# The low parts of the weights in three tiles that begin 128, 256 and 384 bytes past a multiple of 512

## The chip, the cores and the metric

The kernel runs on one NeuronCore of a Trainium2 chip. What counts is the device time of one execution, in microseconds (us). Engines are named as the profile names them: PE is the matrix engine (its matmuls; PEld are its weight loads), DVE the vector engine, ACT the scalar engine, POOL the GpSimd engine, SP the engine that here only issues DMAs. SBUF is the on-chip memory of 128 partitions from which all engines read. Addresses below are bytes within a partition.

## The reference

A decoder trunk of two layers on 256 tokens of width 2048, all in float32:

```
for i in range(2):
    hn = rmsnorm(h, norm_mix[i])
    mix = pool_mixer(hn) if i == 0 else diff_attention(hn)      # layer 0: trailing means and 4 products of 512x512
    h = h + mix                                                 # layer 1: w_qkv [2048, 6144], 8 heads, w_o [2048, 2048]
    hn = rmsnorm(h, norm_ffn[i])
    h = h + (silu(hn @ w_gate[i]) * (hn @ w_up[i])) @ w_down[i] # 2048 -> 5632 -> 2048
return rmsnorm(h, final_norm)
```

Nearly all the work is in the matrix products, and their weights are read once from memory.

## The kernel before

A product in float32 is made of products in a faster, shorter format, `float32r`. A weight block of 128 x 2048 numbers (`raw`, 1 MB, one DMA on SP's queue) is split in `halves` (lines 105 to 110): ACT copies it, rounded, to the high part `whi` (line 108), and DVE subtracts that from `raw` and writes the low part `wlo` (line 109). Activations are split in the same way when they are made, and stay in SBUF as `xp`, `h` or `oT`. A product is then three matmuls: activation high with weight high, activation high with weight low, activation low with weight high. In `group` (line 162), the activations, 128 columns, are the loaded, stationary operand, and 512 columns of `whi` or `wlo` are streamed past it, the moving operand. In `product` (lines 419 and 421, for the queries and keys) it is the other way round: 128 columns of `whi` or `wlo` are loaded and 512 or 256 columns of an activation stream. Each matmul has a weight load of its own.

There are 331 weight blocks: 3 for the pooling mixer, 176 for `w_gu` (the gate and up products), 88 for `w_down`, 32 for `w_qk`, 16 each for `w_v` and `w_o`. Three buffers each of `raw`, `whi` and `wlo` let the DMA, the split and the matmuls of successive blocks run side by side. In three of the eight pairs of row tiles (`SEVEN`), a gate and up product takes seven block products in place of eight; it needs sums of the weight blocks, made on DVE as `tsum` (lines 114 to 117) and split to `thi` and `tlo` (lines 120 and 121), which have one buffer each.

The order of the instructions on each engine is set by the scheduler of the framework in which the kernel is written, which also hands out a pool's buffers in the order in which it thinks they come free. So `whi` and `wlo` of one block always got buffers of the same place in their pools, and the places mostly went round in threes; once in each feed-forward layer, at its sixth block, the block took again the place of the block just before it.

Every large tile of the program as built begins at a multiple of 512 bytes: `raw` at 65024, 73216 and 81408, `whi` at 89600, 97792 and 105984, `wlo` at 114176, 122368 and 130560, and so do `xp`, `h`, `oT`, `tsum`, `thi`, `tlo` and the blocks of 2048 bytes in them that a matmul streams. Some small tiles of the attention do not: `q_c`, `k_s`, `s_sb` and `bias` begin 224 bytes past a multiple of 512, `o_n` 288 past, `a_sb` 32 past.

Of the kernel before, what the change touches and what calls it, by code (L numbers as in the profile page):

```python
# [9 lines left out]
F32 = mybir.dt.float32  # L10
F32R = mybir.dt.float32r
# [5 lines left out]
P = 128  # L17
# [27 lines left out]
def trunk_kernel(ctx, tc, x_t, x_n, gains, scale_in, final_in, subln, lam_in, band, dist,  # L45
# [15 lines left out]
    whl = ctx.enter_context(tc.tile_pool(name="whl", bufs=3))  # L61
# [3 lines left out]
    turn = {"acc": 0, "aux": 0}  # L65
# [8 lines left out]
    def aux(shape=(P, 512)):  # L74
        turn["aux"] += 1
        return bank(5 + turn["aux"] % 3, shape)
# [19 lines left out]
    def f32(ap):  # L96
        return ap.bitcast(F32)


    def load(src):  # L100
        raw = wraw.tile([P, 4, 512], F32, name="raw")
        nc.sync.dma_start(out=raw, in_=src)
        return raw

    def halves(raw, lo_block=0):
        hi = whl.tile([P, 4, 512], F32R, name="whi")
        lo = whl.tile([P, 4, 512], F32R, name="wlo")
        nc.scalar.copy(hi[:, lo_block:], raw[:, lo_block:])  # L108
        nc.vector.tensor_tensor(lo[:, lo_block:], raw[:, lo_block:], f32(hi[:, lo_block:]), ALU.subtract)  # L109
        return hi, lo  # L110
# [17 lines left out]
    def group(steps, seven_pool=None):  # L128
# [15 lines left out]
        for (a, seven, src), step in zip(steps, plan):  # L144
            raw = load(src)
            w = [halves(raw, B11 if seven else 0)]
            if seven:
                w.append(sums(seven_pool, raw))
            for b, parts in step:
                first = b not in ps  # L150
                if first:
                    ps[b] = bank(b)
                for at, which, block in parts:
                    hi, lo = w[which]
                    if seven:
                        ah, al = a[:, 0, at], a[:, 1, at]
                    else:
                        k, t = at
                        ah, al = (a[:, k, i, t * P:(t + 1) * P] for i in range(2))
                    for x, y in ((ah, hi), (ah, lo), (al, hi)):  # L160
                        left[b] -= 1
                        nc.tensor.matmul(ps[b], x, y[:, block], start=first, stop=(left[b] == 0))  # L162
                        first = False
# [235 lines left out]
    with tc.tile_pool(name="attn", bufs=1, reuse_waits="tile") as ap_, ExitStack() as heads:  # L399
        at = heads.enter_context(tc.tile_pool(name="attn_tmp", bufs=2, reuse_waits="tile"))  # L400
# [13 lines left out]
        def product(src, acts):  # L414

            ps = acc((P, 2, S))
            hi, lo = (x.rearrange("p b (u n) -> p (b u) n", n=P) for x in halves(load(src)))
            for k, a in enumerate(acts):
                big = lambda: nc.tensor.matmul(ps.rearrange("p a s -> p (a s)"), hi[:, k], a.rearrange("p a s -> p (a s)"),  # L419
                                               start=(k == 0), stop=(k == NK - 1))  # L420
                small = lambda: nc.tensor.matmul(ps[:, 0, :], lo[:, k], a[:, 0, :], start=False, stop=False)  # L421
                if k < NK - 1:
                    big()
                    small()
                else:
                    small()
                    big()
            return ps

        def transpose_probs(h, probs):  # L430

            a_t = ap_.tile([P, 2, S], F32, name=f"aT{h}")
            tr_ps = aux()
            for qb in range(2):
                for kb in range(qb + 1):
                    o0 = kb * S + qb * P
                    nc.tensor.transpose(tr_ps[:, o0:o0 + P], probs[qb][:, kb * P:(kb + 1) * P], ident)
            nc.scalar.copy(a_t[:, 0, :], tr_ps[:, 0:S])
            nc.scalar.copy(a_t[:, 1, P:], tr_ps[:, S + P:])
            aT.append(a_t)  # L440
# [3 lines left out]
        for h in range(H):  # L444

            if h:
                qk = ap_.tile([P, 4, S], F32, name=f"qk{h}", tag="qk", bufs=8)
            for i in range(4):
                ps = product(w_qk[h * 4 + i], acts)
                if i == 1 and probs is not None:  # L450
                    transpose_probs(h - 1, probs)
                if r is None:
                    bc = aux()
                    for t in range(2):
                        nc.tensor.matmul(bc[:, t * P:(t + 1) * P], r_col[:, t:t + 1].broadcast_to([P, P]), ident,
                                         start=True, stop=True)
                    r = ap_.tile([P, S], F32, name="r_row")
                    nc.scalar.copy(r, bc[:, :S])

                    lp = ap_.tile([P, 2], F32, name="lp")  # L460
                    nc.vector.tensor_tensor(lp, lam_sb[:, 0:2], lam_sb[:, 2:4], ALU.mult)
                    l_ps = aux()
                    nc.tensor.matmul(l_ps[:, 0:2], ones, lp, start=True, stop=True)
                    le = ap_.tile([P, 2], F32, name="le")
                    nc.scalar.activation(le, l_ps[:, 0:2], AF.Exp)
                    neg_lam = ap_.tile([P, 1], F32, name="neg_lam")
                    nc.vector.scalar_tensor_tensor(neg_lam, le[:, 1:2], -LAMBDA_INIT, le[:, 0:1], ALU.add, ALU.subtract)
                    gs = ap_.tile([P, 2], F32, name="gs")
                    nc.vector.tensor_scalar(gs, subln_sb, 1.0 - LAMBDA_INIT, None, ALU.mult)
                c = at.tile([P, S], F32, name="q_c")  # L470
                nc.scalar.copy(c, ps[:, 1, :])
                if i < 2:
                    nc.vector.tensor_tensor(qk[:, i, :], ps[:, 0, :], c, ALU.add)
                else:
                    s = at.tile([P, S], F32, name="k_s", bufs=1)
                    nc.vector.tensor_tensor(s, ps[:, 0, :], c, ALU.add)
                    nc.vector.tensor_tensor(qk[:, i, :], s, r, ALU.mult)
            bias = at.tile([P, 2 * P], F32, name="bias")
            nc.vector.tensor_scalar(bias, dist_sb, -(2.0 ** (-8.0 * (h + 1) / H)), None, ALU.mult)
            probs = []  # L480
            for qb in range(2):
                nk = (qb + 1) * P
                b_ap = bias[:, P:] if qb == 0 else bias
                ps_t, inv = [], []
                for c in range(2):
                    sc = aux()
                    nc.tensor.matmul(sc[:, :nk], qk[:, c, qb * P:(qb + 1) * P], qk[:, 2 + c, :nk], start=True, stop=True)  # L487
                    s = at.tile([P, S], F32, name="s_sb", bufs=3)
                    nc.vector.scalar_tensor_tensor(s[:, :nk], sc[:, :nk], qs_col[:, qb:qb + 1], b_ap, ALU.mult, ALU.add)
                    m = at.tile([P, 1], F32, name="m_neg", bufs=3)  # L490
                    nc.vector.tensor_reduce(m, s[:, :nk], AX.X, ALU.max, negate=True)
                    p = at.tile([P, S], F32, name="p_sb", bufs=4)
                    l = at.tile([P, 1], F32, name="l_sum", bufs=3)
                    nc.scalar.activation(p[:, :nk], s[:, :nk], AF.Exp, bias=m, accum_out=l)
                    iv = at.tile([P, 1], F32, name="l_inv", bufs=4)
                    nc.vector.reciprocal(iv, l)
                    ps_t.append(p)
                    inv.append(iv)
                nc.vector.tensor_tensor(inv[1], inv[1], neg_lam, ALU.mult)
                p1 = at.tile([P, S], F32, name="p1_sb")  # L500
                nc.vector.tensor_scalar(p1[:, :nk], ps_t[1][:, :nk], inv[1], None, ALU.mult)
                a = at.tile([P, S], F32, name="a_sb")
                nc.vector.scalar_tensor_tensor(a[:, :nk], ps_t[0][:, :nk], inv[0], p1[:, :nk], ALU.mult, ALU.add)
                probs.append(a)
        transpose_probs(H - 1, probs)
        heads.close()
        at = heads.enter_context(tc.tile_pool(name="out_tmp", bufs=2, reuse_waits="tile"))
# [132 lines left out]
```

## Time and profile before

| | before |
|---|---|
| median of 3 runs | 1916.08 us (1915.61 to 1916.73) |
| the profiled execution, its own time | 1915.97 us |
| its span, first to last instruction | 1914.2 us |
| PE busy | 1871.7 us, 98% |
| DVE busy | 1344.9 us, 70% |
| ACT busy | 921.3 us, 48% |
| DMA | 358.83 MB, 187 GB/s over the span |

Matmuls overlap in the profile: one of 512 columns is shown some 390 ns long, while the next begins some 227 ns after it. How fast PE works is read from the starts of its matmuls, in the timeline, not from the mean length of one.

### The profile page before, as it was taken

How to read it: one execution, taken by the hardware profiler on the slowest of the kernel's cores; microseconds unless marked ns; L12 is line 12 of the kernel's file. 1: busy time of each engine (PE TensorE's matmuls, PEld its weight loads, DVE VectorE, ACT ScalarE, POOL GpSimd, SP SyncE). 2: the span in 40 equal slices, each digit the busy share in tenths (PEclk: the TensorE clock that was granted, in tenths of full speed). 3: DMA queues.
4: the chain of work that ended last, by engine and by line, in shares of the span. 5: the costliest groups of instructions: out<-in, count | busy, mean ns of one | idle time of the engine just before them, and what ended most of it. 6: DMA issues, size and time to landing. Idle time of an engine off the chain costs nothing.

```text
span 1914.2 us, 20836 instructions
## 1 busy us (share of the span) xinstructions
PE 1871.7 (98%) x8508; PEld 1526.5 (80%) x8508; DVE 1344.9 (70%) x1311; ACT 921.3 (48%) x892; POOL 0.7 (0%) x6
## 2 busy tenths in 40 slices
PE   8899999999999999999999999999999999999997
PEld 5678888888888888888887787788888888888886
DVE  5898756888558975666654356898558897468854
ACT  5555534455434545544445545555434554345543
POOL 0000000000000000000000000000000000000000
PEclk9999999999999999999999999999999999999999
DMA  7455555555556564555553454555555556565552
GB/s 284 154 198 198 197 180 198 195 198 198 195 188 211 176 207 169 177 174 177 174 186 137 139 176 157 189 203 199 198 195 201 198 176 211 185 219 198 198 194 92
DMA packets 51151, 358.83 MB, mean 187 GB/s; under 512 B 6000, under 2 KB 6256, under 8 KB 8432
## 3 DMA queue, kind: packets, MB, share of 16 engines
q1 hardware_dynamic: 50080, 355.36, 53.3%
q10 hardware_dynamic: 976, 2.15, 0.3%
q8 instruction: 66, 1.08, 0.2%
q14 instruction: 29, 0.24, 0.0%
HBM read 355.39 MB, written 2.10 MB: 187 GB/s over the span
## 4 chain that ended last, share of the span: by engine, by line
PE 93%; DVE 3%; ACT 2%; DMA 1%; issue 1%; SPq 0%; DVEq 0%; ACTq 0%
PE b L162 80%; PE b L419 6%; PE b L421 3%; PE b L357 1%; DVE wlo L109 1%; ACT whi L108 1%; DMA x_tok<-x_n 1%; PE b L297 1%; PE b L487 1%; ACT sq L212 0%; PE b L533 0%; PE b L307 0%; DVE xp L224 0%; DMA raw<-w_gu 0%; ACT o_sq L525 0%
## 5 line engine op out<-in xcount | busy, mean ns | idle before, releaser
L109 DVE TENSOR_TENSOR wlo<-raw,whi 128x2048 fp32r<-128x2048 f32 (+1 forms) x331 | 721.3, 2182 | 354.8 <-ACT whi L108 354.0
L108 ACT CAST whi<-raw 128x2048 fp32r<-128x2048 f32 (+1 forms) x331 | 603.1, 1825 | 607.6 <-PE b L162 511.1
L162 PE MATMUL b<-whi,xp 128*128 128x512 f32 x2412 | 768.4, 392 | 6.5 <-DVE xp L224 3.9
L162 PEld LDWEIGHTS b<-whi,xp 128*128 128x128 f32 x2412 | 453.2, 188 | 104.4 <-issue 5.1
L162 PE MATMUL b<-wlo,xp 128*128 128x512 f32 x1206 | 470.7, 390 | 1.8 <-DVE wlo L109 1.8
L162 PE MATMUL b<-whi,h 128*128 128x512 f32 x1408 | 438.3, 391 | 0.0
L162 PEld LDWEIGHTS b<-whi,h 128*128 128x128 f32 x1408 | 263.7, 188 | 56.8 <-DVE h L360 2.1
L162 PE MATMUL b<-wlo,h 128*128 128x512 f32 x704 | 274.2, 390 | 0.1
L162 PEld LDWEIGHTS b<-wlo,xp 128*128 128x128 f32 x1206 | 226.9, 188 | 50.0 <-DVE wlo L109 3.0
L121 DVE TENSOR_TENSOR tlo<-tsum,thi 128x2048 fp32r<-128x2048 f32 x66 | 151.1, 2290 | 52.6 <-ACT thi L120 51.7
L162 PE MATMUL b<-thi,xp 128*128 128x512 f32 x528 | 185.1, 397 | 2.4 <-ACT thi L120 2.3
L419 PE MATMUL b<-xp,whi 128*128 128x512 f32 x512 | 183.1, 402 | 0.0
L120 ACT CAST thi<-tsum 128x2048 fp32r<-128x2048 f32 x66 | 126.1, 1910 | 99.5 <-DVE tsum L117 77.0
L162 PEld LDWEIGHTS b<-wlo,h 128*128 128x128 f32 x704 | 132.2, 188 | 27.3 <-DVE wlo L109 0.5
L421 PE MATMUL b<-xp,wlo 128*128 128x256 f32 x512 | 138.0, 280 | 0.0
L162 PEld LDWEIGHTS b<-thi,xp 128*128 128x128 f32 x528 | 97.2, 189 | 28.7 <-ACT thi L120 10.9
L419 PEld LDWEIGHTS b<-xp,whi 128*128 128x128 f32 x512 | 95.0, 188 | 19.8
L162 PE MATMUL b<-tlo,xp 128*128 128x512 f32 x264 | 105.4, 399 | 0.0
L421 PEld LDWEIGHTS b<-xp,wlo 128*128 128x128 f32 x512 | 96.6, 189 | 2.6
L162 PE MATMUL b<-whi,oT 128*128 128x512 f32 x256 | 81.5, 397 | 0.5 <-DVE xp L224 0.5
L114 DVE TENSOR_TENSOR tsum<-raw 128x1024 f32<-128x1024 f32 x66 | 80.5, 1220 | 0.6
L162 PEld LDWEIGHTS b<-tlo,xp 128*128 128x128 f32 x264 | 50.0, 189 | 13.7 <-DVE tlo L121 3.2
(122 smaller groups left out, 1016.7 us busy)
## 6 DMA issues: line engine op xcount, KB each, us to landing
raw<-w_gu SPq DMA_DIRECT2D x176, 1024.0 KB, 4.8
raw<-w_down SPq DMA_DIRECT2D x88, 1024.0 KB, 4.8
raw<-w_qk SPq DMA_DIRECT2D x32, 1024.0 KB, 4.8
raw<-w_v SPq DMA_DIRECT2D x16, 1024.0 KB, 4.8
raw<-w_o SPq DMA_DIRECT2D x16, 1024.0 KB, 4.8
raw<-pool_w SPq DMA_DIRECT2D x3, 1024.0 KB, 16.9
x_tok<-x_n SPq DMA_DIRECT2D x1, 2048.0 KB, 14.2
xf<-x_t SPq DMA_DIRECT2D x3, 512.0 KB, 10.8
```

What stands on the lines that cost most here:

```text
L108: nc.scalar.copy(hi[:, lo_block:], raw[:, lo_block:])
L109: nc.vector.tensor_tensor(lo[:, lo_block:], raw[:, lo_block:], f32(hi[:, lo_block:]), ALU.subtract)
L114: nc.vector.tensor_tensor(t[:, T1:T3 + 1], raw[:, B11:B22 + 1], raw[:, B12:B12 + 1].broadcast_to([P, 2, 512]), ALU.add)
L120: nc.scalar.copy(hi, t)
L121: nc.vector.tensor_tensor(lo, t, f32(hi), ALU.subtract)
L162: nc.tensor.matmul(ps[b], x, y[:, block], start=first, stop=(left[b] == 0))
L297: nc.tensor.matmul(zp[g][t], u, w[:, k % 4], start=(k % 4 == 0 and i == 0), stop=(k % 4 == 3 and i == 2))
L357: nc.tensor.transpose(tp[:, k, t * P:(t + 1) * P], h[:, t, (2 * i + k) * P:(2 * i + k + 1) * P], ident)
L419: big = lambda: nc.tensor.matmul(ps.rearrange("p a s -> p (a s)"), hi[:, k], a.rearrange("p a s -> p (a s)"), start=(k == 0), stop=(k == N ...
L421: small = lambda: nc.tensor.matmul(ps[:, 0, :], lo[:, k], a[:, 0, :], start=False, stop=False)
L487: nc.tensor.matmul(sc[:, :nk], qk[:, c, qb * P:(qb + 1) * P], qk[:, 2 + c, :nk], start=True, stop=True)
```

## The change

The three buffers of `wlo` become three tiles with a tag of their own, used in turn, and gaps of 128 bytes stand before each of them and behind the last. As built, `wlo_a`, `wlo_b` and `wlo_c` begin at 114304, 122624 and 130944, which is 128, 256 and 384 bytes past a multiple of 512. `raw` and `whi` stay where they were. What lies behind (from `ss` on) moves up by 512 bytes, so that it keeps its place within 512. To make room, the attention's `bias` has one buffer in place of two.

```
+    turn["lo"] = 0
+
     def halves(raw, lo_block=0):
         hi = whl.tile([P, 4, 512], F32R, name="whi")
-        lo = whl.tile([P, 4, 512], F32R, name="wlo")
+        i = turn["lo"] % 3
+        turn["lo"] += 1
+        if turn["lo"] <= 3:
+            whl.tile([P, 32], F32, name=f"gap{i}", tag=f"gap{i}", bufs=1)
+        lo = whl.tile([P, 4, 512], F32R, name="wlo_" + "abc"[i], tag=f"wlo{i}", bufs=1)
+        if turn["lo"] == 3:
+            whl.tile([P, 32], F32, name="gap3", tag="gap3", bufs=1)
         nc.scalar.copy(hi[:, lo_block:], raw[:, lo_block:])
         nc.vector.tensor_tensor(lo[:, lo_block:], raw[:, lo_block:], f32(hi[:, lo_block:]), ALU.subtract)
         return hi, lo
...
-            bias = at.tile([P, 2 * P], F32, name="bias")
+            bias = at.tile([P, 2 * P], F32, name="bias", bufs=1)
```

No instruction is added or removed. The order on the engines is the same but for three places: DVE's `bias` instructions, one a head, come one head later but for the first (still ahead of their readers), and at the start of each feed-forward layer the sixth block's low part, which now goes strictly in turn, gets the buffer of the third block before it instead of the one just freed. There the scheduler puts the low part behind the sums. In the first feed-forward layer DVE's rows were these before (the number at the end of a name is a buffer's; `wlo_644` is the sixth block's, `tsum_612`, `thi_616` and `tlo_617` are the sums of the fifth):

```order
L109 TENSOR_TENSOR wlo_644<-raw_641,whi_643 128x2048 [waits DMAHW4_49,Activation_49]
L114 TENSOR_TENSOR tsum_612<-raw_606 128x1024 [waits DVE_49]
L116 TENSOR_TENSOR tsum_612<-tsum_612,raw_606 128x512 [waits DVE_49]
L117 TENSOR_TENSOR tsum_612<-tsum_612,raw_606 128x512 [waits DVE_49]
L109 TENSOR_TENSOR wlo_674<-raw_671,whi_673 128x2048 [waits DMAHW5_49,Activation_49]
L121 TENSOR_TENSOR tlo_617<-tsum_612,thi_616 128x2048 [waits Activation_49]
L109 TENSOR_TENSOR wlo_704<-raw_701,whi_703 128x2048 [waits DMAHW6_49,Activation_49]
```

And they are these now (numbers of buffers are higher by 4, of lines by 9):

```order
L123 TENSOR_TENSOR tsum_616<-raw_610 128x1024 [waits DVE_49]
L125 TENSOR_TENSOR tsum_616<-tsum_616,raw_610 128x512 [waits DVE_49]
L126 TENSOR_TENSOR tsum_616<-tsum_616,raw_610 128x512 [waits DVE_49]
L118 TENSOR_TENSOR wlo_c_648<-raw_645,whi_647 128x2048 [waits DMAHW4_49,PE_49,Activation_49]
L130 TENSOR_TENSOR tlo_621<-tsum_616,thi_620 128x2048 [waits Activation_49]
L118 TENSOR_TENSOR wlo_a_678<-raw_675,whi_677 128x2048 [waits DMAHW5_49,PE_49,Activation_49]
L118 TENSOR_TENSOR wlo_b_708<-raw_705,whi_707 128x2048 [waits DMAHW6_49,Activation_49]
```

The low part stands three rows later, behind the sums, and it and the next one now wait for PE too, for the matmuls that read their buffers last. PE's rows at the same place before:

```order
L162 MATMUL b5_506<-whi_578,xp_94 128x512
L162 MATMUL b6_486<-wlo_644,xp_96 128x512 [waits DVE_49]
L162 MATMUL b6_486<-whi_643,xp_96 128x512 x2
L162 MATMUL b6_486<-wlo_644,xp_96 128x512
L162 MATMUL b6_486<-whi_643,xp_96 128x512
L162 MATMUL b4_502<-wlo_644,xp_96 128x512
L162 MATMUL b4_502<-whi_643,xp_96 128x512 x2
L162 MATMUL b4_502<-wlo_644,xp_96 128x512
L162 MATMUL b4_502<-whi_643,xp_96 128x512
L162 MATMUL b7_569<-wlo_644,xp_96 128x512
L162 MATMUL b1_490<-thi_616,xp_95 128x512 [waits Activation_49]
```

And now:

```order
L171 MATMUL b5_510<-whi_582,xp_94 128x512
L171 MATMUL b1_494<-thi_620,xp_95 128x512 [waits Activation_49]
L171 MATMUL b2_498<-thi_620,xp_95 128x512
L171 MATMUL b3_502<-thi_620,xp_95 128x512
L171 MATMUL b5_510<-thi_620,xp_95 128x512
L171 MATMUL b6_490<-wlo_c_648,xp_96 128x512 [waits DVE_49]
L171 MATMUL b6_490<-whi_647,xp_96 128x512 x2
L171 MATMUL b6_490<-wlo_c_648,xp_96 128x512
L171 MATMUL b6_490<-whi_647,xp_96 128x512
L171 MATMUL b4_506<-wlo_c_648,xp_96 128x512
L171 MATMUL b4_506<-whi_647,xp_96 128x512 x2
```

The four matmuls on `thi` have moved ahead of those on the low part. The second feed-forward layer has the same exchange at the same place.

## The prediction

> **What bounds the kernel now.** I read the page's head first, then its chain of waits, then the groups.
>
> ```profile
> PE 1871.7 (98%) x8508; PEld 1526.5 (80%) x8508; DVE 1344.9 (70%) x1311; ACT 921.3 (48%) x892; POOL 0.7 (0%) x6
> PE 93%; DVE 3%; ACT 2%; DMA 1%; issue 1%; SPq 0%; DVEq 0%; ACTq 0%
> L109 DVE TENSOR_TENSOR wlo<-raw,whi 128x2048 fp32r<-128x2048 f32 (+1 forms) x331 | 721.3, 2182 | 354.8 <-ACT whi L108 354.0
> L108 ACT CAST whi<-raw 128x2048 fp32r<-128x2048 f32 (+1 forms) x331 | 603.1, 1825 | 607.6 <-PE b L162 511.1
> L162 PE MATMUL b<-wlo,xp 128*128 128x512 f32 x1206 | 470.7, 390 | 1.8 <-DVE wlo L109 1.8
> L162 PE MATMUL b<-wlo,h 128*128 128x512 f32 x704 | 274.2, 390 | 0.1
> L421 PE MATMUL b<-xp,wlo 128*128 128x256 f32 x512 | 138.0, 280 | 0.0
> ```
>
> PE is the bound: 98% busy, 93% of the chain. ACT waits 511.1 us for PE to free `whi`, so the split runs ahead of PE and is paced by it. PE's matmuls on `wlo` waited 1.8 us in all for DVE. A faster or slower line 109 would therefore be hidden; only two things can move the end: the pace of a matmul itself, and the few places where PE waits.
>
> The pace is read from the starts in the timeline of PE's rows. In the steady stretch from 270 to 290 us the groups and the first and last low matmul are:
>
> ```profile
> L162 PE MATMUL b<-whi,h 128*128 128x512 f32 x60 | 18.6, 389 | 0.0
> L162 PE MATMUL b<-wlo,h 128*128 128x512 f32 x30 | 11.7, 389 | 0.0
> 269.86 0.39 PE L162 MATMUL b<-wlo,h 128*128 128x512 f32 x1
> ...
> 289.58 0.39 PE L162 MATMUL b<-wlo,h 128*128 128x512 f32 x1
> ```
>
> There are 30 low matmuls, every third one, so 29 x 3 = 87 matmuls lie between the two starts: 19.72 us / 87 = 226.7 ns. What would the 512 columns alone take? Just after PE's longest wait the granted clock is 0.50 (column after POOL's), and the starts in that stretch give the pace at half clock:
>
> ```profile
> 66.00:68.50 2.50, 2.50 (x7) 1.92 (x7) 1.74 (x7) 1.41 (x2) 0.00 (x0) 0.50 0.26 39
> 66.10 0.63 PE L162 MATMUL b<-wlo,xp 128*128 128x512 f32 x1
> 67.38 0.63 PE L162 MATMUL b<-wlo,xp 128*128 128x512 f32 x1
> 68.66 0.49 PE L162 MATMUL b<-wlo,xp 128*128 128x512 f32 x1
> ```
>
> Six matmuls in 2.56 us, 427 ns each, so 213 ns at full clock. The steady pace is 13.3 ns above that. The excess looks as if it belongs to the weight load, not to the columns: in the queries and keys, where 512 and 256 columns alternate, nine pairs go by in 3.12 us:
>
> ```profile
> 866.67 0.28 PE L421 MATMUL b<-xp,wlo 128*128 128x256 f32 x1
> ...
> 869.79 0.28 PE L421 MATMUL b<-xp,wlo 128*128 128x256 f32 x1
> ```
>
> That is 346.7 ns a pair; 768 columns at 213/512 ns are 320, and 26.7 ns are left for two matmuls, again 13.3 each. And the next weight load runs while the columns stream: at 280.06 us the low matmul and a weight load start together.
>
> ```profile
> 280.06 0.39 PE L162 MATMUL b<-wlo,h 128*128 128x512 f32 x1
> 280.06 0.41 PEld L162 LDWEIGHTS b<-whi,h 128*128 128x128 f32 x2
> ```
>
> So some 13.3 ns of each such matmul are lost to something that the half clock leaves room for. Whether that depends on where in 512 bytes the two reads begin is the whole question, because before, both always begin at 0.
>
> **The change part by part.** *PE reading `wlo` at 128, 256, 384.* In the trace of before no matmul streams a tile that is off a multiple of 512, so this has no row of its own. Low bound: the excess goes away wherever one of the two reads is of `wlo`. These are the 1206 and 704 above, 128 more and 24 of the mixer:
>
> ```profile
> L162 PE MATMUL b<-wlo,oT 128*128 128x512 f32 x128 | 50.4, 394 | 0.0
> L297 PE MATMUL b<-wlo,xp 128*128 128x512 f32 x24 | 10.3, 430 | 1.6 <-DVE wlo L109 1.6
> ```
>
> together 2062 that stream it, and 512 that load it: 2574 x 13.3 ns = 34 us less. High bound: a second excess of the same size, 34 us more; I know no steady row with a larger one. I take 0, for three rows that stand nearest. First, loads of a stationary operand off 512 are in the trace: the transposes of `a_sb` (32 past) have the length of those of `h` (0 past).
>
> ```profile
> L357 PE MATMUL b<-ident,h 128*128 128x128 f32 x176 | 28.6, 278 | 0.1
> L437 PE MATMUL b<-ident,a_sb 128*128 128x128 f32 x24 | 4.1, 272 | 0.0
> ```
>
> They are plain float32, at less than one column a cycle, so they leave the room that the half clock leaves; they weigh little. Second, other engines read and write at 224 and 288 past at the speed of aligned work of the same size: 420 against 420 ns on DVE (line 476 against 245), 474 against 475 on ACT (line 529 against 223).
>
> ```profile
> L476 DVE TENSOR_TENSOR k_s<-b,q_c 128x256 f32<-128x256 f32 x16 | 6.7, 420 | 14.5 <-ACT q_c L471 14.5
> L245 DVE TENSOR_TENSOR e<-e 128x256 f32<-128x256 f32 x6 | 2.5, 420 | 2.3 <-ACT e L243 2.3
> L529 ACT ACTIVATE o_n<-b,rs_r 128x256 f32<-128x256 f32 x16 | 6.5, 474 | 1.5 <-DVE rs_r L206 1.5
> L223 ACT ACTIVATE oT<-b,gs 128x256 fp32r<-128x256 f32 x16 | 7.4, 475 | 3.8 <-PE b L533 2.3 <-DVE oT L224 1.5
> ```
>
> Third, if the engines met in banks of the SBUF that the address selects, PE's pace would move with what DVE and ACT do. In two stretches of 10 us, with DVE busy 9.71 and 4.59, PE starts the same number of matmuls:
>
> ```profile
> 610.00:620.00 10.00, 10.00 (x46) 8.29 (x45) 9.71 (x8) 3.73 (x4) 0.00 (x0) 1.00 0.67 225
> 1040.00:1050.00 10.00, 10.00 (x46) 8.27 (x45) 4.59 (x2) 4.60 (x3) 0.00 (x0) 1.00 0.31 105
> ```
>
> The loss is thus PE's own, between its two reads, and most simply a shared way in, whatever the address.
>
> The Trainium skill goes further ("TensorE: Matmul & The Clock Gate", Part 2, step 1): it gives PE two independent SBUF read ports, and says that the next load takes no read bandwidth from the running matmul. By it the sum for this part is 0 and no address can matter. The trace agrees that the load runs beside the matmul, but not that it is free at full clock: 226.7 against 213 ns.
>
> *DVE writing `wlo`.* By the same DVE rows, nothing per instruction; and what it might cost is covered by the slack before line 108. Should that cover go, each 1% of 721.3 us is 7 us of DVE time, still under 98% of PE.
>
> *The order at the start of each feed-forward layer.* The sixth block's low part must now wait until PE has read the third block's low part for the last time. Before, in the first of the two layers:
>
> ```profile
> 82.33 2.29 DVE L109 TENSOR_TENSOR wlo<-raw,whi 128x2048 fp32r<-128x2048 f32 x1
> 85.88 0.39 PE L162 MATMUL b<-wlo,xp 128*128 128x512 f32 x1
> 87.47 0.39 PE L162 MATMUL b<-whi,xp 128*128 128x512 f32 x1
> 90.31 1.20 PE L162 MATMUL b<-thi,xp 128*128 128x512 f32 x4
> ```
>
> The low part began at 82.33; the last read of the third block's is the matmul at 85.88, over at 86.27. So it begins at 86.3 and ends at 88.6, 4.0 us later. PE needed it at 87.69, the matmul after that of 87.47. Now four matmuls on `thi` stand before it, 4 x 0.227, so PE asks at 88.6: a wait of 0 to 0.2 us. `thi` is ready in time: its sums take over the low part's place on DVE from 82.2 and end near 84.9, ACT's cast (1.9 us) starts when the old `thi` is read, at 85.1, and ends at 87.0, before 87.7. `tlo` follows the low part at 88.5 and is done at 90.8, when PE has worked off its ten matmuls from 88.6, at 90.9. Gone is the wait before the row at 90.31, 0.12 us, and 0.1 us of the slower start behind it. Sum: 0.2 saved, 0 to 0.3 lost, in each of two layers: 0. Behind the low part on DVE stand `tlo` and two more low parts, none needed by PE before 95. On SP's queue two DMAs of `raw` change places there; the blocks they bring are used some 10 us later.
>
> *`bias` with one buffer, the gaps, the shift by 512 bytes.* `bias` is written and read by DVE in turn, so one buffer adds no wait between engines; nothing else moves within 512. 0 us.
>
> The sum is 0 against the profiled execution's own 1915.97 us (span 1914.2 and 1.8 around it), which is 0.1 under the median of the runs; I predict 1916.0.
>
> **The rivals.** *A, faster:* the 13.3 ns are two reads that start together at the same place within 512 bytes and meet line for line; shifted, they no longer do. For it speaks that the loss is constant to the tenth of a ns at every pair of starts, as a fixed phase would make it; against it that the queries and keys, with another rhythm, lose exactly as much. It gives 1916 - 34 = 1882 us if all three offsets help, and 1916 - 34/3 = 1905 if one does. It decides from 1.5 ns a low matmul (3.8 us / 2574).
>
> *B, slower:* a streamed read that starts inside a block of 512 bytes touches one block more, and pays for it as for a load. Nothing in the trace speaks for it but that no such read is there. With 13.3 ns on the 2062 that stream `wlo`, 27 us, 1943; the time is visibly slower from 1.9 ns each.
>
> *C, slower:* the later low part is not covered by the moved `thi`, since ACT or DVE run later there than I place them. The price is at most the delay of 4.0 us in each of two layers, 1924; it decides at 1.9 us a layer. Against it: I found both ends within 0.3 us of PE's need.
>
> **How the numbers follow.** A measurement of this kernel tells about 0.2%, 3.8 us, from no change. No change (1913 to 1919): 0.71. A: 0.15, a third of it near 1905. B: 0.06. C: 0.05. The remaining 0.03 are small gains or losses at places that I did not see, two thirds gains. Faster 0.17, same 0.71, slower 0.12. The range for 8 in 10 takes in, beside no change, the weak form of A and all of C: 1904 to 1925; the likeliest case's own is 1913 to 1919.
>
> **What would show it.** Right: the low matmuls of line 171 in a steady stretch of the feed-forward layer start again at 226.7 ns, the pairs of lines 428 and 430 at 346.7, line 118 has its 2182 ns, and near 88 us PE waits no more than 0.3 us. A would show as low rows after which the next starts 213 to 216 ns later, perhaps at one of `wlo_a`, `wlo_b`, `wlo_c` alone; B as low rows of 229 ns and more; C as a gap of PE before the low matmul near 88.6 and its twin near 1213. Wrong would make me above all that PE streams an operand off 512 differently, which I had no row for.

## The result: slower by 0.4%, and the profile after

The changed kernel took 1922.45 us (1921.71 to 1924.76, six runs), beside 1915.49 us for the kernel before in the same comparison: a ratio of 1.0038, with an interval of 1.0025 to 1.0051. The forecast was no change, 1916.0 us. The time lies inside the range of 1904 to 1925 us that was given, but above the 1913 to 1919 us of no change, and the interval leaves out a ratio of 1.

The head of the changed kernel's profile and the groups of PE on the low parts (busy us, mean ns of one):

```profile
span 1920.4 us, 20834 instructions
PE 1879.3 (98%) x8508; PEld 1526.6 (79%) x8508; DVE 1345.2 (70%) x1311; ACT 920.6 (48%) x892; POOL 0.7 (0%) x6
L171 PE MATMUL b<-wlo_a,xp 128*128 128x512 f32 x404 | 159.8, 395 | 0.0
L171 PE MATMUL b<-wlo_b,xp 128*128 128x512 f32 x400 | 156.0, 390 | 0.9 <-DVE wlo_b L118 0.9
L171 PE MATMUL b<-wlo_c,xp 128*128 128x512 f32 x402 | 159.5, 397 | 0.8 <-DVE wlo_c L118 0.8
```

The span grew by 6.2 us. PE is busy for 7.6 us more, and idle for 1.4 less; DVE and ACT do in the same time what they did. So the loss lies in the matmuls and not in waits, and the three low tiles, which differ in their address alone, do not cost the same. The steady stretch of the forecast, 270 to 290 us, shows it in the starts of the low matmuls, which are every third matmul of PE there (a row begins with the start and the length in us; the dots stand for rows left out; a low matmul and the two high ones behind it are called a three below):

```profile
270.91 0.40 PE L171 MATMUL b<-wlo_c,h 128*128 128x512 f32 x1
...
275.71 0.40 PE L171 MATMUL b<-wlo_c,h 128*128 128x512 f32 x1
276.40 0.40 PE L171 MATMUL b<-wlo_a,h 128*128 128x512 f32 x1
...
281.21 0.40 PE L171 MATMUL b<-wlo_a,h 128*128 128x512 f32 x1
281.89 0.39 PE L171 MATMUL b<-wlo_b,h 128*128 128x512 f32 x1
...
286.65 0.39 PE L171 MATMUL b<-wlo_b,h 128*128 128x512 f32 x1
```

Each block has eight low matmuls, so seven threes between its first and its last. They take 4.80 us on `wlo_c` (384 past a multiple of 512) and 4.81 on `wlo_a` (128 past), 686 to 687 ns for three matmuls, and 4.76 us on `wlo_b` (256 past), 680 ns for three, which is the pace of before (3 x 226.7). With the two high matmuls of a three unchanged, a low one at 128 or 384 has become some 7 ns longer. The tile at 256 pays nothing.

Over the whole trace the starts give the same picture. For matmuls of 512 columns in the group function, intervals over 260 ns (waits and slow clock) left out, the mean interval after one on the low parts was 226.9 ns before; now it is 233.8 on `wlo_a`, 227.0 on `wlo_b`, 233.9 on `wlo_c`. `wlo_a` and `wlo_c` are streamed by 1374 matmuls of that function, and 6.9 ns on each make 9.5 us. The span grew by 6.2 us only, so 3.3 us came back elsewhere, mainly in the intervals over 260 ns in which PE waits. That DVE and ACT have a little more time to be ready would explain this; it was not tested.

### The profile page after: what moved, and what is told of

It reads as the page before. It is cut to its first block, busy times and chain, and to the rows that moved or that the text cites. A ratio compares the mean times of both kernels' runs of the same rounds, so it can differ in the third digit from the quotient of the medians.

```text
span 1920.4 us, 20834 instructions
## 1 busy us (share of the span) xinstructions
PE 1879.3 (98%) x8508; PEld 1526.6 (79%) x8508; DVE 1345.2 (70%) x1311; ACT 920.6 (48%) x892; POOL 0.7 (0%) x6
## 4 chain that ended last, share of the span: by engine, by line
PE 93%; DVE 3%; ACT 2%; DMA 1%; issue 1%; SPq 0%; DVEq 0%; ACTq 0%
PE b L171 80%; PE b L428 6%; PE b L430 3%; PE b L366 1%; ACT whi L117 1%; DMA x_tok<-x_n 1%; PE b L306 1%; PE b L496 1%; DVE wlo_b L118 0%; ACT sq L221 0%; PE b L542 0%; PE b L316 0%; DVE xp L233 0%; DVE y L396 0%; DMA raw<-w_gu 0%
## 5 line engine op out<-in xcount | busy, mean ns | idle before, releaser
L118 DVE TENSOR_TENSOR wlo_a<-raw,whi 128x2048 fp32r<-128x2048 f32 (+1 forms) x111 | 243.4, 2192 | 130.1 <-ACT whi L117 129.1
L118 DVE TENSOR_TENSOR wlo_c<-raw,whi 128x2048 fp32r<-128x2048 f32 (+1 forms) x110 | 240.0, 2181 | 119.3 <-ACT whi L117 116.6
L118 DVE TENSOR_TENSOR wlo_b<-raw,whi 128x2048 fp32r<-128x2048 f32 (+1 forms) x110 | 238.9, 2172 | 109.0 <-ACT whi L117 108.7
L171 PE MATMUL b<-wlo_c,xp 128*128 128x512 f32 x402 | 159.5, 397 | 0.8 <-DVE wlo_c L118 0.8
L171 PE MATMUL b<-wlo_a,xp 128*128 128x512 f32 x404 | 159.8, 395 | 0.0
L171 PE MATMUL b<-wlo_b,xp 128*128 128x512 f32 x400 | 156.0, 390 | 0.9 <-DVE wlo_b L118 0.9
L171 PE MATMUL b<-wlo_c,h 128*128 128x512 f32 x240 | 94.9, 395 | 0.0
L171 PE MATMUL b<-wlo_a,h 128*128 128x512 f32 x240 | 94.7, 395 | 0.0
L171 PEld LDWEIGHTS b<-wlo_c,xp 128*128 128x128 f32 x402 | 75.8, 189 | 17.9 <-DVE wlo_c L118 1.6
L171 PEld LDWEIGHTS b<-wlo_a,xp 128*128 128x128 f32 x404 | 75.9, 188 | 16.8 <-DVE wlo_a L118 0.8
```

## The experiments

Two things had changed at once: the addresses, and the order of the buffers with the exchange at the start of the feed-forward layers. The first four kernels separate them, and ask what about the address counts. The first six kernels below have the instruction order of the changed kernel.

**The turn without the gaps.** The same three tags in turn, all tiles at a multiple of 512:

```
-    whl.tile([P, 32], F32, name=f"gap{i}", ...)     # and gap3
```

> The three low tiles keep their own tags and go in turn, and every instruction stands where it stands in the changed kernel, but there are no gaps: all three begin at a multiple of 512. Theory 1 (the start address of the streamed operand costs): the low matmuls start 226.7 ns apart again and the time is that of before, 1915.5 us within 1.5. Theory 2 (the new order at the start of each feed-forward layer, and the low tiles' new turn, cost): the time stays near 1922.4.

Measured: 1916.83 us beside 1916.27, ratio 1.0002 (0.9993 to 1.001). The new order and the new turn of the buffers cost nothing that can be measured; the gaps are what costs.

**All low tiles at 256.**

```
 gaps in bytes ahead of wlo_a, wlo_b, wlo_c and behind:  128, 128, 128, 128  ->  256, 0, 0, 256
```

> All three low tiles begin 256 past a multiple of 512. Theory 1 in the form that only odd multiples of 128 cost: 226.9 ns a low matmul as wlo_b had it, 1915.5 us within 1.5. If any start off 512 cost something and wlo_b was spared by its neighbours in the turn: 2038 low matmuls at 234 ns, 1926 us.

Measured: 1916.46 us beside 1916.27, ratio 1.0001 (0.9992 to 1.0009), and 227.2 ns after a low matmul. A shift of 256 costs nothing that can be measured.

**All low tiles at 128.**

```
 gaps:  128, 128, 128, 128  ->  128, 0, 0, 384
```

> All three low tiles begin 128 past a multiple of 512. Theory 1: all 2038 low matmuls of the group function at 234.2 ns, so the loss of the changed kernel (7.0 us from two tiles of three) grows by half, to 10.4 us: 1926 us. Theory 2: 1922.4 as in the changed kernel. If the tiles must differ from each other to cost: 1915.5.

Measured: 1932.28 us, ratio 1.0082 (1.0069 to 1.0095), 16 us more than before. All three tiles now have the longer matmuls (the last number before the second bar is the mean ns, stretch of 270 to 290 us; the matmuls on `wlo` and on `whi` had 389 there before):

```profile
L172 PE MATMUL b<-whi,h 128*128 128x512 f32 x58 | 18.2, 395 | 0.0
L172 PE MATMUL b<-wlo_c,h 128*128 128x512 f32 x11 | 4.3, 395 | 0.0
L172 PE MATMUL b<-wlo_b,h 128*128 128x512 f32 x10 | 4.0, 395 | 0.0
L172 PE MATMUL b<-wlo_a,h 128*128 128x512 f32 x8 | 3.2, 395 | 0.0
```

So it is the address and not the tile. The loss was 16 us and not the 10.4 that the changed kernel's loss scaled by half: the interval after a low matmul is as long as there (233.7), but here that after a high one rose too, from 227.1 to 229.0 ns on average, where the changed kernel had 227.1.

The rise is not spread evenly. Two stretches of the same work, the down products on `h` in the first and in the second layer, show it in the first and last low matmul of a block:

```profile
271.63 0.40 PE L172 MATMUL b<-wlo_c,h 128*128 128x512 f32 x1
...
276.53 0.40 PE L172 MATMUL b<-wlo_c,h 128*128 128x512 f32 x1
1663.08 0.40 PE L172 MATMUL b<-wlo_c,h 128*128 128x512 f32 x1
...
1667.89 0.40 PE L172 MATMUL b<-wlo_c,h 128*128 128x512 f32 x1
```

Seven threes take 4.90 us in the one and 4.81 in the other. PE has two rhythms here at the same addresses: a three of 234, 226 and 227 ns, 687 in all, or one of 234, 230 and 236, 700 in all. Most stretches between two waits of PE stay in one of them to the end: of the four longest on `h`, three had a mean of 232.3 to 232.7 ns after the high matmuls, the fourth 226.3. The changed kernel has slow threes too, but only behind waits, and none comes back in the same stretch once a three on `wlo_b`, the tile at 256, has gone by at the fast pace. Here no low tile is at 0 or 256: 558 of the 1758 threes that the trace holds whole took 697 ns or more, where the changed kernel had 74 of 1760. At 13 ns a three these 484 make 6.3 us, which is about what the 16 us have over the expected 10.4. What decides which rhythm PE takes up after a wait, the traces do not show.

**The activations at 128.** This run is to tell whether a place is bad by itself, or only by its distance from the other operand. In the group function the activation is what is loaded while the weights stream.

```
+    resid.tile([P, 32], F32, name="xgap", tag="xgap")      # ahead of xp; 384 bytes behind it
+    hp.tile([P, 32], F32, name="hgap", tag="hgap")         # ahead of the h tiles; the same ahead of qk and oT
 gaps of the low tiles:  0, 128, 128, 256
```

> All activations (xp, h, oT: the loaded operand in the group function, the streamed one in the queries and keys) begin 128 past a multiple of 512; the low tiles begin 0, 128 and 256 past, the high tiles at 0. Theory 1a (absolute: a streamed operand that begins at an odd multiple of 128 costs 7.6 ns, whatever is loaded): only the matmuls on wlo_b run at 234 ns (+5.2 us), those on whi, wlo_a and wlo_c at 227; the 1024 matmuls of queries and keys, which now stream from 128, lose 7.6 ns each (+7.8 us); about 1928 us. Theory 1b (relative: it costs when the streamed and the loaded operand start an odd multiple of 128 apart): wlo_b at 227, and all on whi, wlo_a, wlo_c, thi and tlo at 234, some 6200 matmuls, +47 us; about 1960 us.

Measured: 1941.05 us, ratio 1.0133 (1.0119 to 1.0146), between the two expectations. The groups of PE from 270 to 290 us decide between them:

```profile
L180 PE MATMUL b<-whi,h 128*128 128x512 f32 x59 | 18.5, 393 | 0.0
L180 PE MATMUL b<-wlo_b,h 128*128 128x512 f32 x12 | 4.7, 388 | 0.0
L180 PE MATMUL b<-wlo_c,h 128*128 128x512 f32 x9 | 3.5, 394 | 0.0
L180 PE MATMUL b<-wlo_a,h 128*128 128x512 f32 x8 | 3.2, 395 | 0.0
```

Now `wlo_b`, which begins at 128 like the activations, has the shortest matmuls, and `whi` and `wlo_a`, both at 0, have become long, though nothing about their own place is new. The mean intervals over the whole trace: 227.6 ns after `wlo_b`, 231.8 to 232.6 after the other three. The distance counts, as theory 1b has it; its price was set too high, since the intervals here are 232 and not 234 ns, and part of the 5 ns on each of some 6300 matmuls, 31 us, was covered: the time rose by 25.

**Low tiles at other distances.** Six more places, three to a run:

```
 gaps:  32, 32, 32, 416     (low tiles at 32, 64, 96)
 gaps:  160, 32, 32, 288    (low tiles at 160, 192, 224)
```

> The low tiles begin 32, 64 and 96 past a multiple of 512; activations and high tiles at 0. What is known: the pace goes by the distance of the two reads of PE, 226.9 ns at 0 and 256, 234 at 128 and 384. Theory S (steps: what counts is in which half of 256 bytes each read begins): all three at 226.9 ns, 1916 us. Theory L (the two reads overlap in part, so the cost grows evenly with the distance): 228.7, 230.5 and 232.3 ns, mean 3.6 ns on 2038 low matmuls, 1923.5 us. Theory M (0 and 128 are not the ends of the curve): one of the three below 226.5 ns, and then the same distance for all activations would be worth some us.

> The low tiles begin 160, 192 and 224 past a multiple of 512. Theory S: all three at 234.2 ns, as at 128, 1932 us. Theory L: the mirror image of 96, 64 and 32, that is 232.3, 230.5 and 228.7 ns, 1923.5 us. Theory M: not the mirror image of the run with 32, 64 and 96, and one of the six below 226.5 ns.

Measured: 1938.88 us (ratio 1.012, 1.0103 to 1.0137) and 1938.43 us (1.0118, 1.0103 to 1.0133), slower than any of the three theories said. The mean intervals after the low matmuls were 233.2, 232.3, 231.2 and 231.8, 230.8, 233.6 ns, with no order in the distance that a straight line or a step would have. The further loss is in the neighbours: after matmuls on `whi`, which still begin at 0 as the activations do, the interval was 231.4 and 230.9 ns in place of 227.1. In the first of the two runs, from 270 to 290 us:

```profile
L172 PE MATMUL b<-whi,h 128*128 128x512 f32 x59 | 18.5, 394 | 0.0
L172 PE MATMUL b<-wlo_b,h 128*128 128x512 f32 x11 | 4.3, 394 | 0.0
L172 PE MATMUL b<-wlo_c,h 128*128 128x512 f32 x10 | 3.9, 392 | 0.0
L172 PE MATMUL b<-wlo_a,h 128*128 128x512 f32 x8 | 3.2, 395 | 0.0
```

**Everything at 128.** If only the distance counts, moving both operands must be free.

```
+    resid.tile([P, 32], F32, name="xgap", tag="xgap")      # in the kernel before, ahead of xp, and nothing else
```

> The kernel before with one gap of 128 bytes ahead of the activations: these, the raw blocks, high and low parts, sums and everything behind them begin 128 past a multiple of 512, so that the two reads of PE are again a multiple of 256 apart. Theory 1b (the distance between the streamed and the loaded operand counts): 226.7 ns a matmul and the time of before, 1916 us within 2. Theory 1a (any read that begins at an odd multiple of 128 costs): the 6900 matmuls of the group function at 231 to 234 ns and the 1024 of queries and keys with them, 1945 to 1970 us.

Measured: 1916.39 us beside 1916.13, ratio 1.0004 (0.9994 to 1.0014), and the groups from 270 to 290 us as before:

```profile
span 1913.5 us, 20836 instructions
L164 PE MATMUL b<-whi,h 128*128 128x512 f32 x60 | 18.4, 389 | 0.0
L164 PE MATMUL b<-wlo,h 128*128 128x512 f32 x30 | 11.7, 389 | 0.0
```

So 128 is not a bad place by itself. Theory 1a has fallen.

**High and low part at the same distance.** In the runs with odd distances the distance changed from matmul to matmul. Here it stays the same within a block, and changes from block to block. The high parts now go strictly in turn too, which moves some rows again at the start of each feed-forward layer, the matmuls of the sixth block among them; this was not run without the gaps.

```
-        hi = whl.tile([P, 4, 512], F32R, name="whi")
+        hi = whl.tile([P, 4, 512], F32R, name="whi_" + "abc"[i], tag=f"whi{i}", bufs=1)   # a gap ahead of each pair
```

> High and low part of a block begin at the same place, 32, 64 or 96 past a multiple of 512 by turns, so that within a block the distance between the two reads stays the same. Theory R (a rhythm: the pace settles at 226.7 ns only while the two reads begin at the same place within 256 bytes; at any other distance, constant or not, it stays near 231.5): all three pairs at 230 to 233 ns, some 6150 matmuls, 1945 us. Theory C (changes of the distance from matmul to matmul are what costs, since they alternated in the runs with shifted low tiles alone): 226.7 ns again and 1917 us. Theory M (some constant distance is better than 0): one pair below 226 ns.

> As the run with pairs at 32, 64 and 96, with 160, 192 and 224. Theory R: 230 to 233 ns, 1945 us. Theory C: 226.7 ns and 1917 us. Theory M: one pair below 226 ns.

Measured: 1945.09 us (ratio 1.0153, 1.0132 to 1.0173) and 1951.12 us (1.0184, 1.0164 to 1.0204). The mean intervals after a matmul on a high part were 233.1, 229.9 and 233.1 ns at 32, 64 and 96, and 233.8, 233.2 and 233.3 at 160, 192 and 224; on the low parts they were 230.0 to 235.0. The head of the first shows that the loss is PE's, at the same 98%; the groups are those from 270 to 290 us:

```profile
span 1942.3 us, 20832 instructions
PE 1900.1 (98%) x8508; PEld 1526.8 (79%) x8508; DVE 1347.1 (69%) x1311; ACT 918.2 (47%) x892; POOL 0.7 (0%) x6
L176 PE MATMUL b<-whi_b,h 128*128 128x512 f32 x27 | 8.6, 391 | 0.0
L176 PE MATMUL b<-whi_a,h 128*128 128x512 f32 x16 | 5.2, 395 | 0.0
L176 PE MATMUL b<-whi_c,h 128*128 128x512 f32 x16 | 5.2, 394 | 0.0
```

A constant distance does not help, and none of the seven places off a multiple of 256 is better than 0. Theory R's 1945 us came true for the first run and is 6 us short for the second; theories C and M have fallen. None of these kernels is faster than the one before, so there was no better version to run.

## Why the prediction was wrong

*What bounds the kernel, and where the time could move.* Right. PE has remained the bound at 98%, and of the 9.5 us by which its matmuls grew, 6.2 arrived at the end.

*The loss of 13.3 ns a matmul between PE's two reads.* That it comes from the two reads was argued, and stays so: no place that was tried took it away. What the runs show is that a further loss depends on the two reads together: moving either one against the other costs (ratios 1.0082 and 1.0133), moving both together does not (1.0004).

*"Most simply a shared way in, whatever the address": the step that failed.* Whether the address plays a part was settled from the trace of before, where both reads always began at the same place, and so nothing could show it. Of the three rows that were to stand in for it, none could have: the transposes are plain float32 and take 162 ns each for 128 columns (28.6 us for 176), which leaves room between reads; DVE and ACT are other engines, and no part of what happened here; and that PE's pace did not change with DVE's work excludes that the engines collide, not that PE's own two reads do. The term "PE reading `wlo`" was taken as 0; it measured 6.9 ns on 1374 low matmuls, 9.5 us, of which 6.2 reached the end. The bounds, 34 us either way, held it.

*Rival A* came nearest to the cause, two reads whose places count together, and had the wrong sign: it took the equal start for the bad case. *Rival B* had the sign, and a price of 13.3 ns where it is 6.9, on two tiles of three; its mechanism, a streamed read that pays for beginning inside a block, has fallen with the run that moved everything by 128. The forecast gave the two 0.15 and 0.06. A resource that the trace shows in one state only deserved more than 0.21 for the other states, and when it loses something at a fixed rate, the sign of a change to it was open.

*Rival C and the order at the start of the feed-forward layers.* The sum of 0 was right. Around 88 us the changed kernel shows:

```profile
85.86 2.29 DVE L118 TENSOR_TENSOR wlo_c<-raw,whi 128x2048 fp32r<-128x2048 f32 x1 [2.21 <-PE b L171]
87.20 1.07 PE L171 MATMUL b<-thi,xp 128*128 128x512 f32 x4
88.20 0.50 PE L171 MATMUL b<-wlo_c,xp 128*128 128x512 f32 x1
```

The low part waits for PE, as was worked out, for 2.2 us; PE works off the four matmuls on `thi`, which take until 87.20 + 4 x 0.227 = 88.11, and starts the low one at 88.20: 0.1 us lost, where up to 0.2 was allowed. The run with the turn and no gaps confirms it for the whole kernel (ratio 1.0002). The prediction also had two DMAs change places on SP's queue. They do not: the blocks come in the order of before, and only the buffers of `raw` in which they land differ.

*DVE writing the shifted tiles.* Right: the three low tiles' groups have means of 2192, 2172 and 2181 ns where the one group had 2182, at other shares of the shorter form.

```profile
L118 DVE TENSOR_TENSOR wlo_a<-raw,whi 128x2048 fp32r<-128x2048 f32 (+1 forms) x111 | 243.4, 2192 | 130.1 <-ACT whi L117 129.1
L118 DVE TENSOR_TENSOR wlo_c<-raw,whi 128x2048 fp32r<-128x2048 f32 (+1 forms) x110 | 240.0, 2181 | 119.3 <-ACT whi L117 116.6
L118 DVE TENSOR_TENSOR wlo_b<-raw,whi 128x2048 fp32r<-128x2048 f32 (+1 forms) x110 | 238.9, 2172 | 109.0 <-ACT whi L117 108.7
```

## What to carry to other kernels

Where PE is the bound and every `float32r` matmul has a weight load of its own, let the streamed and the loaded tiles begin at the same place within 256 bytes: here that was worth up to 1.8% of the time, and a small tile allocated between the big ones can undo it without a trace in the instruction order. When an operand's place is changed, ask what else is read at the same time, and do not take a pace that the trace shows in one state only as independent of that state. And to find such a cost, give several buffers of one ring different places in one run: the same work, side by side, shows which places cost. It does not show what moving all of them would cost: here two tiles of three cost 7 us, and all three 16; the third, at 256, is the likely reason, since the slow rhythm ends with it.

## What the runs showed of the hardware

Matmuls of 512 `float32r` columns, each with a weight load of 128 columns running under the one before, settle at starts some 227 ns apart when the streamed and the loaded operand begin a multiple of 256 bytes apart (0 or 256); with 0 apart that held with both at 0 and with both at 128. At 128 or 384 apart between aligned neighbours the interval is 234 ns; with all matmuls but those on one low tile 128 or 384 apart it is 232; at 32, 64, 96, 160, 192 and 224 apart it lies between 230 and 235 ns, and where the neighbours are aligned they are drawn up to 231 as well. In the kernel before, PE shows intervals of 229 to 236 ns too, but nearly only for the first 15 or so matmuls after it has waited; then it settles. It looks as if equal starts let the two reads fall into step, and other distances keep them out of it; that the changed kernel's slow threes end with a block on `wlo_b` fits this. It is an argument from the numbers: what the reads collide in, why a distance of 128 leaves two steady rhythms, one of which leaves the aligned neighbours alone, and why 32 leaves no such rhythm, these runs do not show.

The Trainium skill ("SBUF — State Buffer", section "Who interferes with whom") gives PE two independent read ports, one for the moving operand and one for the weight load, and says that PE never waits on anyone. No run here shows PE waiting for another engine's reads. But its two reads are not independent at this pace: 227 against 232 to 234 ns by their distance alone.

In the queries and keys, where the low tile is what is loaded and 512 and 256 columns alternate, the sign is the other one: the mean interval after the 512 columns was 232.9 ns before and is 230.6 with the loaded low tile at 128. On 512 pairs that is about a microsecond, too little for these runs to tell as a time; the change was not tried there alone.
